# One decoder layer step: the last convolution tile beside the attention heads, no paged attention beside the fourth head, weight remainders in halves

## The chip, the cores and the metric

The kernel runs on one core of one Trainium2 chip. The core has a matrix engine (PE, with PEld for its weight loads), a vector engine (DVE), a scalar engine (ACT), a general engine (POOL) and queues for DMA, of which SP issues nearly all. Each engine works through its own instructions in a fixed order and waits on semaphores for the others. The metric is the device time of one launch in microseconds (us), the median of several runs.

## The reference

One layer of a hybrid decoder for a prompt of 1024 tokens (with 16 learned meta tokens ahead of it) and, beside it, one new token for each of 8 sequences that have 4096 tokens in a paged cache. All of it is fp32.

```python
proj = rms_norm(x, ln_mix_pre) @ w_in          # (1040, 1024) @ (1024, 2560)
q, k, v, a, g = split(proj)                    # 512 columns each
u = a * sigmoid(g)
o = softmax(q1 k1') v - lam * softmax(q2 k2') v   # 4 heads, two maps each, causal, ALiBi
y = silu(layer_norm(depthwise_conv31(u) + b))  # 512 channels, causal
x = x + rms_norm(concat(head_norm(o), y) @ w_out, ln_mix_post)
h = rms_norm(x, ln_ffn_pre)
y_prompt = x + rms_norm((silu(h @ w_gate) * (h @ w_up)) @ w_down, ln_ffn_post)
# the 8 sample rows: the same layer, with attention over k, v = cache[page_table]
```

## The kernel before

**Stages.** Every fp32 matmul is done as three matmuls of rounded parts (`mm3`, lines 149 to 151): a weight tile is cast by ACT to its upper part H (L138) and another engine subtracts H from it for the remainder L (L140). The prompt's normalised rows lie transposed in `xH`, `xL` (8 tiles of 128 channels, in three token chunks of 280, 384 and 384). Then come, on PE: the four channel tiles of the convolution group (`stripe_ag(ct)`: two projections `pa` and `pg` from weight tiles `wi12+ct` and `wi16+ct`, the sigmoid on ACT, the product u on DVE); v, q and k of head 0; 32 attention blocks, 8 for each of the 4 heads; the output projection (8 `c_block`s, matmuls `mo`); and the feed-forward part (`pg`, `pu`, `dn`), which takes the rest of the time.

**The depthwise convolution** of a channel tile (`conv_half`, two halves of 512 tokens) is 31 taps: 11 of them are multiplied on ACT (L411, L413) and added on POOL (L414), the other 20 are fused multiply-adds on DVE (L415, L423), and L421 adds the two sums. `conv_norm` (8 token blocks: transposes on PE, statistics on DVE, affine on ACT) and `conv_act` (8 pieces: transposes `zT`, then Silu on ACT, L450) follow later, and write the result to DRAM (`mixT`), from where the output projection reads it (`mx`).

**One attention block** (`attn(h, i)`): scores S on PE (L507, L508), maximum with the ALiBi bias on DVE (`nm`, L509), exponential on ACT (L515), its combination on DVE (L521 to L526), transposes `AT` on PE copied out by ACT (L538), values `o` on PE (L548), then a norm that needs a power on POOL (`or`, L564) and a scaling on ACT (L566).

**What stands beside the blocks.** A generator `chunks()` gives out the projections of the heads to come, 30 pieces, one projection of one token chunk each; the loop calls for as many as `chunk_to` says, the last one by block 22 (`fend`). `dec_step(rate)` moves the paged attention of the 8 sample rows on by so many steps; a step loads a pair of key pages, multiplies them by the query on POOL (L680, twice) and sums on DVE (L690), and later multiplies by value pages on PE (L732). `rate_b` holds a rate for each head, `rate_c` that of the output projection. `dec_max` and `dec_exp` close the scores of one sample row (`dg` is a maximum over partitions on POOL, L707; L712 subtracts it). `cn` is the block at which `conv_norm` begins, `scn` that of the sample rows' convolution. From block 27 on, two tiles of `w_out` are split for each block (`wo0` to `wo7`).

**What sets the order.** The program is written in the order of these loops, but a list scheduler of the framework places the instructions of each engine by priority (the place in the program) and by its own idea of when their inputs are ready. `conv_half` has its priority lowered by 400 places, so its multiply-adds fill in where nothing else is ready. The order of the `w_in` loads on SP is a list (`order`). There are 35 buffers of weight-tile size (`slabs`), so loads wait for buffers to come free.

Of the kernel before, what the change touches and what calls it, by code (L numbers as in the profile page):

```python
# [8 lines left out]
F32 = mybir.dt.float32  # L9
# [11 lines left out]
DB = 8  # L21
# [20 lines left out]
SLAB = 1056  # L42
OHW = P + 4
# [3 lines left out]
def tile_layer(ctx: ExitStack, tc: tile.TileContext, I, O, cfg):  # L47
# [87 lines left out]
    def load_split(src, name, l_eng, n3=True):  # L135
        raw = early.pop(name, None) or load_raw(src, name, n3)
        H = slab(name + "H", F32R)
        S.copy(H[:, :1024], raw[:, :1024])  # L138
        L = slab(name + "L", F32R)
        l_eng.tensor_tensor(L[:, :1024], raw[:, :1024], H[:, :1024].bitcast(F32), op=ALU.subtract)  # L140
        return H, L
# [43 lines left out]
    def xchunk(c):  # L185
# [11 lines left out]
        for k, pt in enumerate(pts):  # L197
            wk = wpre[:, k : k + 1]
            S.mul(xH[k][:, c0 : c0 + w], pt[:, :w], wk)
            V.scalar_tensor_tensor(  # L200
                xL[k][:, c0 : c0 + w], pt[:, :w], wk, xH[k][:, c0 : c0 + w].bitcast(F32), op0=ALU.mult, op1=ALU.subtract
            )
            if c == 0:
                V.tensor_scalar(xsT[:, k, :], pt[:, 0:DB], wk, None, op0=ALU.mult)
# [4 lines left out]
    order = [12, 16, 13, 17, 14, 18, 15, 19, 8, 0, 4, 9, 1, 5, 10, 2, 6, 11, 3, 7]  # L209
# [135 lines left out]
    def stripe_ag(ct):  # L345
# [6 lines left out]
        for c in range(3):  # L352
# [8 lines left out]
            else:  # L361
                d0 = 14 + c0 - DB
                V.tensor_tensor(ut[:, d0 : d0 + w], oa[:, :w], sg[:, :w], op=ALU.mult)

# [382 lines left out]
    def dec_units():  # L747
# [5 lines left out]
        def softmaxes(all_=False):  # L753
# [5 lines left out]
            while exped < ready and (all_ or nk >= at[exped] + cfg["elag"]):  # L759
                dec_exp(exped, st)  # L760
                exped += 1
# [510 lines left out]
    for ct in range(4):  # L1272
        stripe_ag(ct)
        conv_tail_out(ct)
        if ct == cfg["cst"]:
            att_consts()
            lam_consts()
            dec_consts()
        if ct == cfg["sq"]:
            sample_q()  # L1280
        with tc.high_priority(offset=-cfg["conv"]):
            conv_half(ct, 1)
            conv_half(ct, 0)
# [6 lines left out]
    def chunks():  # L1290
        for h in range(NH):
            if h:
# [6 lines left out]
    total = 30  # L1299
# [30 lines left out]
    for n in range(NH * NB):  # L1330
        h, i = n // NB, n % NB
        chunk_to(max(9 * h + (1 if i < 2 else 2 if i < 5 else 3), 1 + int(29 * n / cfg["fend"])))
# [58 lines left out]
    vgrp=2, fing=5, ml_g=0, fend=22, cst=0, db=3, cn=6, scn=12, wo0=27, wor=2, c0=7,  # L1391
    at=8, slabs=35, kv=4, p=6, dve_mul=0, rate_b=(1, 1.25, 1, 0.75), rate_c=1, rate_d=2.45, rate_s=2.2,
# [42 lines left out]
```

## Time and profile before

| | |
|---|---|
| three runs | 1431.78, 1434.7 and 1438.51 us; median 1434.7 |
| the profiled execution | 1440.69 us, of which the span in the trace is 1438.8 |
| mean granted clock of PE | 0.977 |
| busy in the span | PE 1357.1 us (94%), DVE 860.9 (60%), POOL 595.2 (41%), ACT 551.2 (38%) |

PE is busy 94% of the span, so a reader looks for the stretches in which it is not, and then for the engine or wait that PE waits for there. The table of stretches ([rows 1] below) does that for the part in front of the feed-forward stage. Within a stretch the rows of the timeline show single instructions: start, duration, engine, line, operation, tiles, and in square brackets how long the engine had stood idle and what ended that.

### The profile page before, as it was taken

What the parts mean: (1) busy time and instruction counts of PE and PEld (TensorE: products, weight loads), DVE (VectorE), ACT (ScalarE), POOL (GpSimd) and SP (SyncE); (2) the same over time, 40 slices, a digit from 0 to 9 for tenths busy, and PEclk for the clock granted to TensorE, in tenths of its full rate; (3) what the DMA queues carried; (4) which work ended last, traced back from release to release, by engine and by line L of the source; (5) the groups of instructions that cost most, each with busy time, mean ns of one, the idle gap of its engine ahead of it and who ended that gap; (6) DMA issues with size and microseconds to landing.
All of it is one profiled execution on the core that took longest, in us unless ns stands there. A gap on an engine that the chain in (4) does not pass through costs nothing.

```text
span 1438.8 us, 21552 instructions
## 1 busy us (share of the span) xinstructions
PE 1357.1 (94%) x6960; PEld 1057.1 (73%) x6960; DVE 860.9 (60%) x1403; ACT 551.2 (38%) x1112; POOL 595.2 (41%) x479
## 2 busy tenths in 40 slices
PE   5999899989869999999999989999999989999997
PEld 5999799979747787777776757676776765666666
DVE  5689996936684567566645465654653374452158
ACT  6566878797764345113021121312121112211122
POOL 4598867445372113745545455464530000000023
PEclk9999999999889999999999999999999999999999
DMA  8211015226535548678867857777677656763454
GB/s 246 86 59 38 27 55 163 75 96 192 170 98 193 171 148 269 211 259 260 262 226 235 265 199 249 235 257 264 204 263 221 214 163 218 229 190 125 147 195 172
DMA packets 199677, 264.34 MB, mean 184 GB/s; under 512 B 16423, under 2 KB 99816, under 8 KB 199557
## 3 DMA queue, kind: packets, MB, share of 16 engines
q1 hardware_dynamic: 188912, 254.40, 54.3%
q10 hardware_dynamic: 10653, 8.57, 1.8%
q8 instruction: 55, 0.90, 0.3%
q14 instruction: 57, 0.47, 0.1%
HBM read 245.92 MB, written 17.48 MB: 183 GB/s over the span
## 4 chain that ended last, share of the span: by engine, by line
PE 59%; SPq 3%; DMA 3%; issue 3%; DVE 3%; POOL 2%; ACT 1%; POOLq 0%; DVEq 0%; ACTq 0%
PE dn L149 5%; PE pu L149 5%; PE dn L150 5%; PE dn L151 5%; PE pu L151 5%; PE pu L150 5%; PE pg L149 5%; PE pg L150 5%; PE pg L151 5%; PE pv L732 4%; PE mo L151 2%; PE mo L149 2%; PE mo L150 2%; DMA v<-in_cache_v 2%; SPq L665 2%
## 5 line engine op out<-in xcount | busy, mean ns | idle before, releaser
L680 POOL TENSOR_TENSOR k<-k,qB 128x512 f32<-128x512 f32 x256 | 353.5, 1409 | 230.2 <-DMA k<-in_cache_k 176.3
L690 DVE TENSOR_REDUCE s<-k 128x16 f32<-128x1024 f32 x128 | 154.8, 1213 | 101.1 <-POOL k L680 100.9
L956 ACT CAST wH<-wr 128x1024 fp32r<-128x1024 f32 x66 | 69.0, 1048 | 239.4 <-DVE wL L958 124.6
L149 PE MATMUL dn<-wH,aH 128*128 128x512 f32 x352 | 141.3, 405 | 5.0 <-DVE y L999 3.4
L149 PE MATMUL pu<-hH,wH 128*128 128x512 f32 x352 | 141.2, 401 | 1.1 <-DVE y L999 1.1
L150 PE MATMUL dn<-wL,aH 128*128 128x512 f32 x352 | 140.9, 400 | 0.0
L151 PE MATMUL pu<-hH,wL 128*128 128x512 f32 x352 | 139.2, 396 | 1.6 <-DVE wL L958 1.6
L151 PE MATMUL dn<-wH,aL 128*128 128x512 f32 x352 | 140.7, 400 | 0.0
L149 PE MATMUL pg<-hH,wH 128*128 128x512 f32 x352 | 140.4, 399 | 0.0
L150 PE MATMUL pu<-hL,wH 128*128 128x512 f32 x352 | 140.1, 398 | 0.0
L150 PE MATMUL pg<-hL,wH 128*128 128x512 f32 x352 | 139.3, 396 | 0.0
L151 PE MATMUL pg<-hH,wL 128*128 128x512 f32 x352 | 139.2, 395 | 0.0
L958 DVE TENSOR_TENSOR wL<-wr,wH 128x1024 fp32r<-128x1024 f32 x66 | 93.7, 1420 | 46.3 <-ACT wH L956 22.2
L999 DVE TENSOR_TENSOR y<-dn,y 128x512 f32<-128x512 f32 x144 | 95.5, 684 | 38.0 <-PE dn L151 37.1
L414 POOL TENSOR_TENSOR cb<-cb 128x512 f32<-128x512 f32 x80 | 102.9, 1316 | 18.0 <-ACT cb L413 9.9
L1071 POOL TENSOR_TENSOR y<-y,wfpost 128x512 f32<-128x512 f32 x10 | 17.6, 1772 | 206.7 <-ACT ft L1069 206.6
L423 DVE SCALAR_TENSOR_TENSOR acc<-u,cw,acc 128x512 f32<-128x512 f32 x144 | 98.7, 747 | 0.2
L982 ACT CAST aH<-sg 128x512 fp32r<-128x512 f32 x44 | 27.3, 620 | 167.6 <-DVE sg L975 167.5
L149 PEld LDWEIGHTS dn<-wH,aH 128*128 128x128 f32 x352 | 67.5, 192 | 31.8 <-DVE y L999 6.8
L149 PEld LDWEIGHTS pu<-hH,wH 128*128 128x128 f32 x352 | 66.4, 189 | 29.4 <-issue 12.9
L975 DVE TENSOR_TENSOR sg<-sg,pu 128x512 f32<-128x512 f32 x44 | 30.1, 683 | 94.0 <-PE pu L151 94.0
L149 PEld LDWEIGHTS pg<-hH,wH 128*128 128x128 f32 x352 | 66.1, 188 | 27.4 <-issue 11.6
(581 smaller groups left out, 2969.5 us busy)
## 6 DMA issues: line engine op xcount, KB each, us to landing
k<-in_cache_k SPq DMA_DIRECT2D x256, 256.0 KB
v<-in_cache_v SPq DMA_DIRECT2D x256, 256.0 KB
wr<-in_w_gate SPq DMA_DIRECT2D x22, 512.0 KB
wr<-in_w_up SPq DMA_DIRECT2D x22, 512.0 KB
wr<-in_w_down SPq DMA_DIRECT2D x22, 512.0 KB
sd<-in_w_down SPq DMA_DIRECT2D x22, 512.0 KB
sw_gate<-in_w_gate SPq DMA_DIRECT2D x20, 512.0 KB
sw_up<-in_w_up SPq DMA_DIRECT2D x20, 512.0 KB
```

The lines of the kernel that those rows point to most:

```text
L149: T.matmul(out, lhsT=wH, rhs=xH, start=first, stop=False)
L150: T.matmul(out, lhsT=wH, rhs=xL, start=False, stop=False)
L151: mark(T.matmul(out, lhsT=wL, rhs=xH, start=False, stop=last))
L414: G.tensor_tensor(accp, accp, t, op=ALU.add)
L423: V.scalar_tensor_tensor(dst, src, cw[:, ct, k : k + 1], acc, op0=ALU.mult, op1=ALU.add)
L680: x = G.tensor_tensor(kt[:, i, :], kt[:, i, :], qB, op=ALU.mult)
L690: x = V.tensor_reduce(s.rearrange("p a c -> p (a c)"), kt.rearrange("p a (c d) -> p (a c) d", d=HD), axis=AX.X, op=ALU.add)
L732: x = T.matmul(pv[32 * g : 32 * g + 8, :], lhsT=a[:, q + i, :], rhs=vt[:, i, :], start=q + i < 4, stop=q + i >= NPG - 4, tile_position=(0, ...
L956: S.copy(H[:, :1024], raw[:, :1024])
L958: V.tensor_tensor(L[:, :1024], raw[:, :1024], H[:, :1024].bitcast(F32), op=ALU.subtract)
L975: V.tensor_tensor(sg, sg, o, op=ALU.mult)
L999: V.tensor_tensor(y[b][:, ws], o, y[b][:, ws], op=ALU.add)
```

## The change

1. The channel tile ct = 3 leaves the row of four and becomes three more pieces of `chunks()` (33 in all) ahead of the projections of head 2; its convolution follows its third piece, and its weights (15 and 19) are loaded behind tile 5.
2. `rate_b` of the last head goes from 0.75 to 0, `rate_c` from 1 to 1.75 (six steps out of the last head, six into the output projection). `dec_exp` waits for the end of the attention blocks where it isn't asked for all.
3. `conv_norm` begins at block 14 rather than 6, `conv_act` therefore at 22 rather than 14; the sample rows' convolution is called at 14 rather than 12.
4. Where POOL makes a remainder (`w_out` and all of `w_in` but tiles 8 to 12) it does so in two instructions of 512 columns.
5. The sample rows' `xsT` is made from `xH` + `xL` by eight additions behind the loop, not in it.

```diff
--- before.py
+++ after.py
@@ -40,6 +40,7 @@
 C0 = CHUNKS[0][1]
 KT = [(0, META)] + [(META + P * i, P) for i in range(NB)]
 SLAB = 1056
+LATE = {2: 3}
 OHW = P + 4
 
 
@@ -137,7 +138,9 @@
         H = slab(name + "H", F32R)
         S.copy(H[:, :1024], raw[:, :1024])
         L = slab(name + "L", F32R)
-        l_eng.tensor_tensor(L[:, :1024], raw[:, :1024], H[:, :1024].bitcast(F32), op=ALU.subtract)
+        for a in (0, 512) if l_eng is G else (0,):
+            e = a + 512 if l_eng is G else 1024
+            l_eng.tensor_tensor(L[:, a:e], raw[:, a:e], H[:, a:e].bitcast(F32), op=ALU.subtract)
         return H, L
 
     point = {}
@@ -200,13 +203,14 @@
             V.scalar_tensor_tensor(
                 xL[k][:, c0 : c0 + w], pt[:, :w], wk, xH[k][:, c0 : c0 + w].bitcast(F32), op0=ALU.mult, op1=ALU.subtract
             )
-            if c == 0:
-                V.tensor_scalar(xsT[:, k, :], pt[:, 0:DB], wk, None, op0=ALU.mult)
+        if c == 0:
+            for k in range(8):
+                V.tensor_tensor(xsT[:, k, :], xH[k][:, 0:DB].bitcast(F32), xL[k][:, 0:DB].bitcast(F32), op=ALU.add)
 
     w_in_v = I["w_in"][0].rearrange("(k p) n -> p k n", p=P)
 
     ahead = {}
-    order = [12, 16, 13, 17, 14, 18, 15, 19, 8, 0, 4, 9, 1, 5, 10, 2, 6, 11, 3, 7]
+    order = [12, 16, 13, 17, 14, 18, 8, 0, 4, 9, 1, 5, 15, 19, 10, 2, 6, 11, 3, 7]
 
     def w_in_src(ft):
         return w_in_v[:, :, ft * P : (ft + 1) * P]
@@ -361,6 +365,19 @@
             else:
                 d0 = 14 + c0 - DB
                 V.tensor_tensor(ut[:, d0 : d0 + w], oa[:, :w], sg[:, :w], op=ALU.mult)
+            if c < 2:
+                yield
+        conv_tail_out(ct)
+        if ct == cfg["cst"]:
+            att_consts()
+            lam_consts()
+            dec_consts()
+        if ct == cfg["sq"]:
+            sample_q()
+        with tc.high_priority(offset=-cfg["conv"]):
+            conv_half(ct, 1)
+            conv_half(ct, 0)
+        yield
 
 
     cw = cst.tile([P, 4, CW], F32, name="cw")
@@ -756,7 +773,7 @@
                 dec_max(ready, st)
                 at.append(nk)
                 ready += 1
-            while exped < ready and (all_ or nk >= at[exped] + cfg["elag"]):
+            while exped < ready and (all_ or kv_n[1] and nk >= at[exped] + cfg["elag"]):
                 dec_exp(exped, st)
                 exped += 1
 
@@ -1270,17 +1287,9 @@
     xchunk(2)
     conv_consts()
     for ct in range(4):
-        stripe_ag(ct)
-        conv_tail_out(ct)
-        if ct == cfg["cst"]:
-            att_consts()
-            lam_consts()
-            dec_consts()
-        if ct == cfg["sq"]:
-            sample_q()
-        with tc.high_priority(offset=-cfg["conv"]):
-            conv_half(ct, 1)
-            conv_half(ct, 0)
+        if ct not in LATE.values():
+            for _ in stripe_ag(ct):
+                pass
     att_fixed()
     for _ in stripe_v(0):
         pass
@@ -1289,6 +1298,8 @@
 
     def chunks():
         for h in range(NH):
+            if h in LATE:
+                yield from stripe_ag(LATE[h])
             if h:
                 yield from stripe_v(h)
                 yield from stripe_q(h)
@@ -1296,7 +1307,11 @@
 
     fl = chunks()
     emitted = [0]
-    total = 30
+    total = 30 + 3 * len(LATE)
+
+    def keys_at(h):
+        return 9 * h + 3 * len([x for x in LATE if x <= h])
+
 
     def chunk_to(n):
         while emitted[0] < min(n, total):
@@ -1329,7 +1344,7 @@
     nwo, ncb = 0, 0
     for n in range(NH * NB):
         h, i = n // NB, n % NB
-        chunk_to(max(9 * h + (1 if i < 2 else 2 if i < 5 else 3), 1 + int(29 * n / cfg["fend"])))
+        chunk_to(max(keys_at(h) + (1 if i < 2 else 2 if i < 5 else 3), 1 + int((total - 1) * n / cfg["fend"])))
         attn(h, i)
         if cfg["cn"] <= n < cfg["cn"] + NB:
             conv_norm(n - cfg["cn"])
@@ -1388,8 +1403,8 @@
     lag=7, rlag=1, elag=2,
     xn_g=(), wi_first=1, wi_e=(13, 17), sq=0,
     behind=-400, w0=7, w1=7, wi_n=1, anchor=1, wi_v=(8, 9, 10, 11, 12), taps=11, conv=400, r2_g=1, hb=5,
-    vgrp=2, fing=5, ml_g=0, fend=22, cst=0, db=3, cn=6, scn=12, wo0=27, wor=2, c0=7,
-    at=8, slabs=35, kv=4, p=6, dve_mul=0, rate_b=(1, 1.25, 1, 0.75), rate_c=1, rate_d=2.45, rate_s=2.2,
+    vgrp=2, fing=5, ml_g=0, fend=22, cst=0, db=3, cn=14, scn=14, wo0=27, wor=2, c0=7,
+    at=8, slabs=35, kv=4, p=6, dve_mul=0, rate_b=(1, 1.25, 1, 0), rate_c=1.75, rate_d=2.45, rate_s=2.2,
     ffn_l=lambda nc: nc.vector,
 )
 _INS = [
```

On PE, the place where the third channel tile ends. `xH`, `xL` are the prompt's rows, `pa` and `pg` the two projections of a channel tile, `pv` the v projection of a head (tile 8 belongs to head 0). Before:

```order
L149 MATMUL pg_1111<-xH_101,wi18H 128x384
L150 MATMUL pg_1111<-xL_109,wi18H 128x384
L151 MATMUL pg_1111<-xH_101,wi18L 128x384
L149 MATMUL pa_1242<-xH_94,wi15H 128x280
L150 MATMUL pa_1242<-xL_102,wi15H 128x280
L151 MATMUL pa_1242<-xH_94,wi15L 128x280
```

The same place after:

```order
L152 MATMUL pg_1116<-xH_101,wi18H 128x384
L153 MATMUL pg_1116<-xL_109,wi18H 128x384
L154 MATMUL pg_1116<-xH_101,wi18L 128x384
L152 MATMUL pv_1246<-xH_94,wi8H 128x280
L153 MATMUL pv_1246<-xL_102,wi8H 128x280
L154 MATMUL pv_1246<-xH_94,wi8L 128x280
```

The v projection of head 0 follows at once; `pa_..<-xH_94,wi15H` and what belongs to it stands further down, behind the first scores of head 1 (`S`, lines now numbered 17 higher):

```order
L524 MATMUL S_0_2425<-R_10_2188,L_10_1934 128x144
L524 MATMUL S_0_2430<-R_11_2189,L_11_1935 128x144
L152 MATMUL pa_2491<-xH_94,wi15H 128x280
L153 MATMUL pa_2491<-xL_102,wi15H 128x280
L565 MATMUL o_1894<-vm,metaT_115 128x128
L565 MATMUL o_1894<-V_1325,ats_2137 128x128 x3
L565 MATMUL o_1894<-V_1325,ats_2145 128x128 x4
L525 MATMUL S_0_2425<-R_10_2190,L_10_1934 128x144
L154 MATMUL pa_2491<-xH_94,wi15L 128x280
```

The 144 matmuls of the fourth tile's two projections have moved there from the place ahead of head 0, and lie among the instructions of attention blocks.

On ACT, a place in the last head, blocks 4 and 5 (`p`: exponentials of a block's two maps; `woNH`: casts of `w_out`; `oh`, `mo`: the norm of a finished block and its result; `u<-zT`: Silu of `conv_act`). Before:

```order
L515 ACTIVATE p_5176,l_4873<-p_5176,nm_5175 128x784
L138 CAST wo4H<-wo4r 128x1024
L515 ACTIVATE p_5185,l_4873<-p_5185,nm_5175 128x784
L566 ACTIVATE oh_4834<-oh_4834,or_4841 128x128 x4
L515 ACTIVATE p_5269,l_4873<-p_5269,nm_5268 128x912
L538 COPY metaT_117<-AT_4982 16x128
L573 ACTIVATE mo_4932<-oT_4927,sublnT 128x512
L138 CAST wo5H<-wo5r 128x1024
```

After:

```order
L467 ACT_TABLE_LOAD
L467 ACTIVATE u_2489<-zT_4741,clnb,clnw 128x512
L139 CAST wo4H<-wo4r 128x1024
L532 ACT_TABLE_LOAD
L532 ACTIVATE p_5185,l_4888<-p_5185,nm_5184 128x912
L583 ACTIVATE oh_4849<-oh_4849,or_4856 128x128 x4
L467 ACT_TABLE_LOAD
L467 ACTIVATE u_2489<-zT_4747,clnb,clnw 128x512
L532 ACT_TABLE_LOAD
L532 ACTIVATE p_5194,l_4888<-p_5194,nm_5184 128x912
L139 CAST wo5H<-wo5r 128x1024
```

Two of the eight Silus stand between exponentials there, each with an `ACT_TABLE_LOAD` ahead of it and another ahead of the next exponential. In the whole order six Silus with twelve such loads now stand behind the first exponential of the last head, and two with four just ahead of it, in blocks 6 and 7 of head 2. Before, the eight Silus and their loads stood between block 6 of head 1 and block 3 of head 2, and there was no load in the last head.

On POOL, the last head (`k`: products of the paged attention; `woNL`: remainders of `w_out`; `or`: the power in a block's norm). Before:

```order
L140 TENSOR_TENSOR wo5L<-wo5r,wo5H 128x1024
L680 TENSOR_TENSOR k_14_5090<-k_14_5090,qB_4070 128x512 x2
L140 TENSOR_TENSOR wo6L<-wo6r,wo6H 128x1024
L680 TENSOR_TENSOR k_16_5242<-k_16_5242,qB_4070 128x512
L140 TENSOR_TENSOR wo7L<-wo7r,wo7H 128x1024
L564 TENSOR_TENSOR or_5072<-ssq_4874,mhalf 128x4
L680 TENSOR_TENSOR k_16_5242<-k_16_5242,qB_4070 128x512
L564 TENSOR_TENSOR or_5433<-ssq_4874,mhalf 128x4
```

After:

```order
L143 TENSOR_TENSOR wo5L<-wo5r,wo5H 128x512 x2
L143 TENSOR_TENSOR wo6L<-wo6r,wo6H 128x512 x2
L143 TENSOR_TENSOR wo7L<-wo7r,wo7H 128x512 x2
L581 TENSOR_TENSOR or_5034<-ssq_4889,mhalf 128x4
L581 TENSOR_TENSOR or_5328<-ssq_4889,mhalf 128x4
L126 TENSOR_TENSOR zr_r<-zr_t,mhalf 128x1
L126 TENSOR_TENSOR hr_r<-hr_t,mhalf 128x1
```

The products k_14 and k_16 have left, and each remainder is two instructions. Of the eight products and four sums (L690) that stood in this head, four and two are left, both near its beginning; the value matmuls that PE did before the output projection (four) are gone from there, and the output projection has twelve in place of eight.

## Rows read from the trace of the kernel before

**Rows 1.** Stretches: length; PE, PEld, DVE, ACT, POOL busy (instructions); PE clock, DMA share, GB/s.

```profile
153.40:228.60 75.20, 68.12 (x430) 65.20 (x431) 71.21 (x157) 63.57 (x147) 50.66 (x43) 0.95 0.20 63
228.60:297.80 69.20, 68.63 (x479) 67.20 (x478) 52.23 (x132) 57.10 (x156) 38.74 (x35) 1.00 0.37 116
297.80:375.00 77.20, 70.79 (x476) 66.77 (x475) 36.81 (x92) 69.05 (x165) 39.60 (x32) 0.96 0.42 134
375.00:442.20 67.20, 44.34 (x258) 38.56 (x256) 48.70 (x118) 41.95 (x111) 33.52 (x20) 0.77 0.47 153
442.20:528.00 85.80, 85.80 (x402) 68.33 (x401) 48.01 (x85) 33.13 (x90) 18.79 (x21) 1.00 0.49 158
```

**Rows 2.** Timeline of PE: first matmuls of tile 15 and of v of head 0.

```profile
101.48 0.29 PE L149 MATMUL pa<-xH,wi15H 128*128 128x280 f32 x1
...
124.62 0.29 PE L149 MATMUL pv<-xH,wi8H 128*128 128x280 f32 x1
```

**Rows 3.** Groups on DVE to 300 us, the convolution: busy, mean ns, idle before.

```profile
L423 DVE SCALAR_TENSOR_TENSOR acc<-u,cw,acc 128x512 f32<-128x512 f32 x144 | 98.7, 747 | 0.2
...
L423 DVE SCALAR_TENSOR_TENSOR u<-u,cw,acc 128x512 f32<-128x512 f32 x8 | 5.9, 740 | 0.0
L415 DVE TENSOR_SCALAR acc<-u,cw 128x512 f32<-128x512 f32 x8 | 5.8, 746 | 0.0
L421 DVE TENSOR_TENSOR acc<-acc,cb 128x512 f32<-128x512 f32 x8 | 5.5, 690 | 4.2 <-POOL cb L414 4.2
```

**Rows 4.** Groups on DVE in head 0 (153.4 to 228.6 us).

```profile
L423 DVE SCALAR_TENSOR_TENSOR acc<-u,cw,acc 128x512 f32<-128x512 f32 x44 | 30.8, 744 | 0.0
```

**Rows 5.** Timeline of PE: the start of its work.

```profile
17.66 0.57 PE L149 MATMUL pa<-xH,wi12H 128*128 128x280 f32 x1 [3.21 <-DVE xsT L204]
```

**Rows 6.** Timeline of ACT about the first Silu.

```profile
290.60 0.51 ACT L298 CAST R<-kT 64x384 fp32r<-64x384 f32 x1
291.13 1.28 ACT L450 ACT_TABLE_LOAD   x1
292.43 0.78 ACT L450 ACTIVATE u<-zT,clnb,clnw 128x512 f32<-128x512 f32 x1
...
295.70 1.28 ACT L515 ACT_TABLE_LOAD   x1
296.99 1.17 ACT L515 ACTIVATE p<-p,nm 128x1040 f32<-128x1040 f32 x1
```

**Rows 7.** Stretches of the last head, columns as in rows 1.

```profile
375.20:424.50 49.30, 32.64 (x176) 27.31 (x174) 39.08 (x109) 31.18 (x81) 24.41 (x15) 0.76 0.42 130
424.50:442.20 17.70, 11.50 (x80) 11.05 (x80) 9.43 (x10) 10.58 (x33) 9.12 (x6) 0.81 0.64 217
```

**Rows 8.** Waits in the last head (375 to 442.2 us): in total, times, longest.

```profile
ACT p L515 <- DVE nm L509: 12.0, 4, 5.6
```

**Rows 9.** Timeline of DVE, POOL and ACT in the last head.

```profile
390.61 0.43 DVE L712 TENSOR_TENSOR s<-s,dg 128x264 f32<-128x264 f32 x1 [4.55 <-POOL dg L707]
402.27 1.22 DVE L690 TENSOR_REDUCE s<-k 128x16 f32<-128x1024 f32 x1 [4.85 <-POOL k L680]
...
429.48 2.92 POOL L140 TENSOR_TENSOR wo7L<-wo7r,wo7H 128x1024 fp32r<-128x1024 f32 x1
432.37 1.01 POOL L564 TENSOR_TENSOR or<-ssq,mhalf 128x4 f32<-128x4 f32 x1
...
433.41 1.28 ACT L566 ACTIVATE oh<-oh,or 128x128 f32<-128x128 f32 x4 [3.74 <-POOL or L564]
```

**Rows 10.** Groups on POOL: key products to 450 us, a remainder in the last head.

```profile
L680 POOL TENSOR_TENSOR k<-k,qB 128x512 f32<-128x512 f32 x51 | 66.2, 1316 | 17.8 <-DMA k<-in_cache_k 17.5
...
L140 POOL TENSOR_TENSOR wo6L<-wo6r,wo6H 128x1024 fp32r<-128x1024 f32 x1 | 2.4, 2355 | 1.0 <-ACT wo6H L138 1.0
```

**Rows 11.** The value matmuls of the paged attention: ns min/median/max, first and last start.

```profile
L732 PE MATMUL pv<-v,s x512: 589/593/1061, 423.3 to 1134.9; 128*8 128x512 f32 x171
```

## The prediction

> **What bounds the kernel now.** I read the page first (PE busy 94% of the span), then the table of stretches, then PE's and ACT's timelines where PE idles. [rows 1] are the stretches that the change touches, cut at the first score matmul of each head. From 442 us on PE has no gap, in the output projection and nearly none in the feed-forward part, so there only PE's own work counts. Head 1 is the same: PE 68.6 of 69.2 us. Head 0 is bound by DVE, 71.2 of 75.2 us (95%), since the convolution's multiply-adds run beside it [rows 4]; PE idles 7.1 us and its mean clock falls to 0.95 of full speed, 2.4 GHz. In head 2 it is ACT, 69.0 of 77.2 us. In the last head no engine is full: PE 44.3, DVE 48.7, ACT 42.0 and POOL 33.5 of 67.2 us, at clock 0.77, because no projection is left to fill in. Its length is a chain of waits: exponentials wait for maxima (12.0 us in four waits, [rows 8]), and DVE twice stands for POOL, 4.55 us for `dg` and 4.85 us for a key product [rows 9].
>
> So the tile that moves doesn't save PE any work. It can only gain where PE idles now, and must not make another engine full where it goes.
>
> **The change part by part.** The sum is made against the profiled execution, 1440.7 us, which lies 6.0 us above the median of the runs, 1434.7.
>
> *The fourth tile leaves the start.* Its matmuls stand between 101.48 and 124.62 us on PE without a gap [rows 2]; v of head 0 follows at once: -23.2 us. Its weight loads go behind tile 5 on SP, past the loads of tiles 8, 0, 4, 9, 1 and 5, which come earlier; nothing on PE waits for them in head 0 before, so I count no gain. `xsT`: the first matmul waits 3.21 us for the last of the in-loop instructions [rows 5]. It doesn't read `xsT`, so what ends its wait is the remainder made just before on the same engine; eight tiny operations leave that row. -0.3, between -1 and +0.5.
>
> *Head 0, 75.2 us.* In it DVE does 44 multiply-adds of the convolution, 30.8 us [rows 4]. A tile has 115.9/4 = 29.0 us of DVE [rows 3]; it was queued behind three others, so with one tile less, and the others begun earlier by 23 us of PE time only, the order puts some 17 us less on DVE between head 0's first scores and head 1's. DVE falls to about 54. PE then bounds: 68.1 us busy, plus one projection piece more (33 pieces spread over the 22 blocks in place of 30; 23.2/6 = 3.9 us a piece), less what the clock gives back (0.05 of 68 = 3.4): 68.6. I take 68.2, -7.0. If nothing of the idle went, +3.9; if all went and the piece hid in it, -11.
>
> *Head 1, 69.2 us.* It gives out twelve pieces where it had eleven, and three of them are double: PE +4 pieces, 15.5 us, to 84.7. To DVE come the tile's 29.0 us and some 2.8 net of other work (sums and a remainder in, three blocks of `conv_norm` out): 52.2 + 31.8 = 84.0. The two are level, and the nearest row for a stage with DVE this full is head 0: it ran DVE at 95%. 84.0/0.947 = 88.7, so +19.5. Ends: +15.5 if PE alone bounds, +31.8 if DVE's work adds on (DVE had 17 us free, but in the wrong places). ACT gets the tile's 22 multiplications, at most 0.78 each like a Silu of the same shape [rows 6], 57.1 + 17 = 74; POOL 20 additions at 1.32 like a key product [rows 10], 38.7 + 26 = 65. Both stay under 88.
>
> *Head 2, 77.2 us.* ACT loses four Silus (3.1 us) and gains the affine part of five blocks of `conv_norm`, 20 short operations by the order, under 10 us by the 0.51 of a wider cast [rows 6]. Loads of the function table stay about as many. Its PE work is even: one piece more, most of the Silus' transposes out. ACT 69 and some 5 more in 77.2: +1, between -5 and +6.
>
> *The last head, 67.2 us.* Out go two key sums on DVE, four products on POOL (4 x 1.32 us), and with them the 4.85 us wait, since the remaining product now stands ahead of the first remainder, not behind it. `dg` stays, and its wait. In come six Silus and twelve loads of the function table on ACT. The row: a load takes 1.28 us, begins as the cast before it ends (290.60 + 0.51 = 291.11) and the next function starts behind it with 0.01 us between [rows 6]. So 6 x 0.78 + 12 x 1.28 = 20.1 us. They all stand between the head's first exponential and its last; that stretch has ACT busy 31.2 of 49.3 us now [rows 7], so 51.3 after: ACT, which waits 18 us there now, becomes the engine that bounds. If waits worth another 2 us are left, the stretch is 53 (+4). In the 17.7 us behind it the key product and the 2.92 us remainder ahead of `or` shrink or go: ACT waits 3.74 us for it [rows 9], -3. With the shorter instructions on POOL, for which DVE need not stand as long, -1. Sum 0; between -9 (ACT's work falls into the waits) and +17 (none does). The convolution's part of `mixT` is now written near this head's end, and the first `mo` matmuls read it; no row of before has a wait there, and I leave it inside the +17.
>
> The Trainium skill's "ScalarE: Activation LUTs" (What ACT_TABLE_LOAD costs) speaks against this part: each switch of table costs the load and a drain, about 2.66 us. By that the twelve would be 32 us, not 15, and the last head some 17 us longer; the rows show no time for a drain, so the sum stays with the row.
>
> *Remainders in halves.* One of 1024 columns takes 2.36 us and a product of 512 columns 1.32 [rows 10]: two halves would be 2.6, +0.3 each on an engine that is 50 to 56% busy in heads 1 to 3 [rows 1]: 0, between -1 and +1 apart from the last head.
>
> *Output projection.* PE is full, so its four extra value matmuls count in whole: 4 x 0.593 = +2.4 us [rows 11]. Six steps of products and sums (POOL 6 x 2.6, DVE 6 x 1.2) lie in engines that are 22% and 56% busy. The feed-forward part does what is left of the paged attention as before: 0, within 2.
>
> Sum: -23.2 - 0.3 - 7.0 + 19.5 + 1 + 0 + 2.4 = -7.6, hence 1433.1 us against the profiled execution and, 6.0 lower, **1427** against the median.
>
> **The rivals.**
> *Exchange.* Head 1 becomes DVE-bound in whole and takes +29 (the tile's own DVE time) where I have 19.5, so that what is saved at the start is paid there: sum +2, 1437, no change. For it: head 0 shows just this with four tiles. Against it: in head 1 DVE has 17 us free, and no convolution is behind it.
> *The table loads (slower).* In the last head the Silus fall on the path of the exponentials in place of its waits: each switch pair holds back an exponential by 3.35 us, the maxima behind it wait for buffers, and the 18 us of waiting stay. +17 there, sum +9, 1444. For it: an engine works in order, and the waits come from DVE, POOL and `dg`, not from ACT. It decides once 8 us more of the 20.1 stand on the path than the 4 that I counted.
> *All gaps close.* Head 0 -11, head 1 +15.5, head 2 -3, last head -6, output projection +2.4: sum -25.6, 1409. For it: PE does no more than before and had 36 us of gaps in heads 0, 2 and 3. Against it: those of the last head come from dependences that the change leaves.
> *It doesn't do what it says.* The order keeps four products and two sums in the last head at rate 0; by this only half the paged attention leaves it. In the sum that is already so.
>
> **How the numbers follow.** 0.5% of 1434.7 is 7.2 us, about what can be told from no change: faster is under 1427.5, slower over 1441.9. Forecast 0.50 (its own range 1419 to 1436, about half of it faster by over 0.5%: 0.27 faster, 0.23 same); exchange 0.19 (0.15 same, 0.04 slower); table loads 0.17 (0.05 same, 0.12 slower); all gaps close 0.14 (faster). That gives faster 0.41, same 0.43, slower 0.16. The range 1413 to 1442 holds the forecast and the exchange, half of the two others.
>
> **What would show it.** In the profile after, v of head 0 should begin at about 101 us on PE; head 0 should take 66 to 71 us with PE over 92% busy and DVE about 55; head 1 85 to 93 us with DVE and PE both over 90%; the last head should hold twelve loads of 1.28 us on ACT, ACT about 60 of 67 us busy, and no wait of DVE for a key product over 2 us. It is wrong if head 1 is over 95 us, if the last head is over 73, or if a load on ACT comes with idle time ahead of it that nothing releases.

## The result and the profile after

The changed kernel is slower: 1459.2 us median (1457.55 to 1461.78) against 1435.7 for the kernel before beside it, a ratio of 1.0145 with a 95% interval from 1.0104 to 1.0186. That is 23.5 us more, where 7.6 less was forecast, and 17 us above the range's upper end.

The stretches of the profiled execution after (span 1455.9), cut in the same places, with columns as in [rows 1]:

```profile
126.98:198.03 71.05, 67.18 (x432) 65.63 (x433) 54.32 (x128) 53.84 (x130) 45.89 (x39) 0.98 0.22 70
198.03:307.08 109.05, 95.14 (x616) 91.96 (x615) 83.47 (x168) 72.68 (x176) 64.86 (x54) 0.95 0.33 104
307.08:381.70 74.62, 67.91 (x460) 64.49 (x460) 46.51 (x122) 63.50 (x168) 42.52 (x41) 0.96 0.25 79
381.70:456.68 74.98, 46.72 (x273) 41.66 (x271) 40.72 (x108) 67.91 (x136) 30.17 (x24) 0.75 0.39 136
456.68:543.00 86.32, 86.32 (x405) 67.91 (x404) 48.23 (x84) 32.59 (x89) 23.55 (x25) 1.00 0.55 182
```

The stages start and end at the first score matmul of a head and at the first `mo`, as before; what other work lies between two such cuts can move. Lengths in us, before (153.44, 228.59, 297.80, 375.32, 442.19 and 1438.8 are the cuts, exact to the matmul; [rows 1] rounds some of them), forecast change and measured change:

| stage | before | forecast | after | change |
|---|---|---|---|---|
| start, to the first score of head 0 | 153.4 | -23.5 | 127.0 | -26.5 |
| head 0 | 75.2 | -7.0 | 71.1 | -4.1 |
| head 1 | 69.2 | +19.5 | 109.0 | +39.8 |
| head 2 | 77.5 | +1 | 74.6 | -2.9 |
| last head | 66.9 | 0 | 75.0 | +8.1 |
| output projection to the end | 996.6 | +2.4 | 999.2 | +2.6 |

The sum is +17.0 in these two executions: the profiled one of before lay 5.0 us above its median, that of after 1.7 below. Five of the six terms lie within 4 us, or within the bounds given for them, of what was forecast; head 1 misses by 20. It is 107.5 to 109.3 us long in the profiles of all six kernels with the late tile and 35 buffers, and 69.2 to 71.2 in all seven with the tile at the start. The small terms are less certain: from profile to profile the start varies by 3 to 4 us and the last stage by 8 to 10. On PE's timeline v of head 0 begins here, where it began at 124.62 [rows 2]:

```profile
98.83 0.29 PE L152 MATMUL pv<-xH,wi8H 128*128 128x280 f32 x1
```

Head 1 splits in two halves (columns as before):

```profile
198.03:230.00 31.97, 31.97 (x223) 31.89 (x223) 11.10 (x26) 26.42 (x62) 19.17 (x17) 1.00 0.36 112
230.00:300.00 70.00, 60.55 (x375) 57.92 (x374) 65.51 (x132) 40.81 (x96) 43.49 (x35) 0.93 0.30 95
```

For 32 us PE is full and DVE works 11.1; for the next 70 DVE is nearly full (65.5) and PE works 60.6 with its clock down to 0.93. The tile's `pa` and `pg` come first, and its taps can't start before `u` is there. The timeline of DVE shows both: at 229.75 it has stood 6.09 us for a score matmul, the last product `u` follows at 230.25, and ten us later nearly every step of an attention block has a tap of 0.74 us ahead of it (L367 makes `u`, L440 is the tap, L526 the maximum).

```profile
229.75 0.57 DVE L526 CUSTOM_DVE_ANT_0 p<-S,alibi 128x400 f32<-128x400 f32 x1 [6.09 <-PE S L525]
...
230.25 0.55 DVE L367 TENSOR_TENSOR u<-pa,sg 128x384 f32<-128x384 f32 x1
...
239.09 0.42 DVE L526 CUSTOM_DVE_ANT_0 p<-S,alibi 128x264 f32<-128x264 f32 x1
239.44 0.74 DVE L440 SCALAR_TENSOR_TENSOR acc<-u,cw,acc 128x512 f32<-128x512 f32 x1
240.10 0.42 DVE L526 CUSTOM_DVE_ANT_0 p<-S,alibi 128x264 f32<-128x264 f32 x1
```

PE's waits in head 1 after (in total, times, longest); before it had one of 0.6 us there:

```profile
PE AT L551 <- DVE nm L526: 4.4, 1, 4.4
PE S L524 <- ACT R L303: 4.0, 1, 4.0
PE S L524 <- DVE L L274: 2.2, 1, 2.2
PE pk L152 <- DVE nm L526: 1.8, 1, 1.8
```

PE stands 13.9 us there in all. The 4.0 us for `R` (the keys of head 2, cast by ACT) lie at the head's end. Before, 24 matmuls of head 3's `v` stood between head 2's keys and its first score:

```profile
297.67 0.29 PE L151 MATMUL pv<-xH,wi11L 128*128 128x280 f32 x1
297.80 0.23 PE L507 MATMUL S<-R,L 128*128 128x144 f32 x1
```

After, no projection is left to put there:

```profile
307.08 0.49 PE L524 MATMUL S<-R,L 128*128 128x144 f32 x1 [4.03 <-ACT R L303]
```

By the code the loop has called for 22 of 30 pieces at block 16 before, one more than head 2's keys need, and for 24 of 33 after, just those.

PE also has more to do in head 1 than the tile. Its projection matmuls go from 265 to 361, the 96 more that four pieces are. But matmuls of attention blocks have moved in too, 16 of the values `o` from head 0's stretch and 30 from head 2's, with 15 transposes `AT`. The largest group of them before, and after:

```profile
L548 PE MATMUL o<-V,ats 128*128 128x128 f32 x46 | 6.4, 275 | 0.0
L565 PE MATMUL o<-V,ats 128*128 128x128 f32 x86 | 13.1, 305 | 0.0
```

In the last head ACT is busy 67.9 of 75.0 us. Its loads there are 15, with seven Silus, where the sum had twelve and six behind the first exponential. The loads, and a piece of the timeline: a load of the function table, the Silu, two short steps with no load ahead of them, a load, the exponential.

```profile
L532 ACT ACT_TABLE_LOAD x8 | 10.3, 1283 | 0.1
L467 ACT ACT_TABLE_LOAD x7 | 9.0, 1283 | 0.1
```

```profile
412.31 1.28 ACT L467 ACT_TABLE_LOAD   x1
413.60 0.78 ACT L467 ACTIVATE u<-zT,clnb,clnw 128x512 f32<-128x512 f32 x1
414.28 0.30 ACT L579 ACTIVATE junk<-oh 128x129 f32<-128x129 f32 x1
414.48 0.19 ACT L579 ACTIVATION_READ_ACCUMULATOR junk<-oh 128x1 f32 x1
414.69 1.28 ACT L532 ACT_TABLE_LOAD   x1
415.98 0.84 ACT L532 ACTIVATE p<-p,nm 128x656 f32<-128x656 f32 x1
```

A load costs its 1.28 us, with at most 0.02 us of idle time ahead of it and behind it in all 15, as the sum took it. The drain that the Trainium skill's "ScalarE: Activation LUTs" (What ACT_TABLE_LOAD costs) adds to it isn't in this trace: by its 2.66 us a switch the 15 loads would be an estimated 40 us, and they take 19.3.

### The profile page after: what moved, and what is told of

The parts are those of the page before. It is cut to its first block, busy times and chain, and to the rows that moved or that the text cites. A ratio compares the mean times of both kernels' runs of the same rounds, so it can differ in the third digit from the quotient of the medians.

```text
span 1455.9 us, 21588 instructions
## 1 busy us (share of the span) xinstructions
PE 1360.9 (93%) x6960; PEld 1061.4 (73%) x6960; DVE 860.8 (59%) x1403; ACT 565.0 (39%) x1124; POOL 601.9 (41%) x502
## 4 chain that ended last, share of the span: by engine, by line
PE 53%; SPq 5%; issue 4%; DMA 4%; DVE 3%; POOL 2%; ACT 1%; POOLq 0%; DVEq 0%; ACTq 0%
PE dn L152 5%; PE dn L153 4%; PE pu L152 4%; PE dn L154 4%; PE pu L154 4%; PE pu L153 4%; PE pg L152 4%; PE pg L154 4%; PE pg L153 4%; PE pv L749 3%; SPq L682 2%; SPq L676 2%; PE mo L152 2%; PE mo L153 2%; DMA k<-in_cache_k 2%
## 5 line engine op out<-in xcount | busy, mean ns | idle before, releaser
L707 DVE TENSOR_REDUCE s<-k 128x16 f32<-128x1024 f32 x128 | 155.0, 1212 | 84.7 <-POOL k L697 84.2
L973 ACT CAST wH<-wr 128x1024 fp32r<-128x1024 f32 x66 | 69.2, 1048 | 241.8 <-DVE wL L975 138.3
L431 POOL TENSOR_TENSOR cb<-cb 128x512 f32<-128x512 f32 x80 | 102.6, 1310 | 25.0 <-ACT cb L430 22.2
L440 DVE SCALAR_TENSOR_TENSOR acc<-u,cw,acc 128x512 f32<-128x512 f32 x144 | 99.7, 747 | 0.2
```

Of the source, the lines that this page charges most:

```text
L431: G.tensor_tensor(accp, accp, t, op=ALU.add)
L440: V.scalar_tensor_tensor(dst, src, cw[:, ct, k : k + 1], acc, op0=ALU.mult, op1=ALU.add)
L707: x = V.tensor_reduce(s.rearrange("p a c -> p (a c)"), kt.rearrange("p a (c d) -> p (a c) d", d=HD), axis=AX.X, op=ALU.add)
```

## The experiments

Each gives the difference to the kernel before that ran beside it, whose median was 1435.7 to 1438.1. Where a ratio says more it stands with its interval. The edits show the lines that matter; others are left out. Two changed kernels that are compared ran at different times, and the kernel before had moved by up to 2.4 us between these, so a few us between them say nothing.

**The parts alone.** The late convolution (`cn=14, scn=14` in the kernel before):

```diff
-vgrp=2, fing=5, ml_g=0, fend=22, cst=0, db=3, cn=6, scn=12, wo0=27
+vgrp=2, fing=5, ml_g=0, fend=22, cst=0, db=3, cn=14, scn=14, wo0=27
```

> The kernel before with one part of the change: conv_norm begins at block 14 and the sample rows' convolution at 14, so that the eight Silus come late (by its order eight Silus with sixteen table loads from block 7 of head 2 to block 7 of head 3). The fourth tile stays at the start, the rates are those of before. Theory A (of the 23.5 us, the last head's 8 come from the Silus and their loads on ACT, which becomes full there): the last head takes 75 to 80 us in place of 67, ACT over 65 us busy in it; head 2 loses some of its 77 us; time 1438 to 1446. Theory B (the last head got longer by the missing paged attention and the moved tile, the loads lie in waits): last head 67 to 69, time 1433 to 1437.

Measured 1435.3, ratio 0.9984 (0.9949 to 1.0020): no difference. Heads 2 and last of this run:

```profile
295.75:362.85 67.10, 62.57 (x429) 58.96 (x427) 47.61 (x125) 56.15 (x158) 39.74 (x36) 1.00 0.31 100
362.85:441.25 78.40, 50.66 (x294) 41.41 (x292) 49.07 (x113) 70.31 (x140) 32.71 (x21) 0.76 0.50 168
```

Both theories were half right. The last head does take 78 us, with ACT busy 70.3 of them; but head 2 gives back 10 of them, since the same Silus and loads are gone from there. Together the two take 145.5 us, before 144.4. The time of the whole run is theory B's, not theory A's.

The rates, the remainders with `xsT`, and the tile alone (edits as in the change's parts 2, 4 and 5, and 1 with 3):

```diff
-rate_b=(1, 1.25, 1, 0.75), rate_c=1,
+rate_b=(1, 1.25, 1, 0), rate_c=1.75,
-while exped < ready and (all_ or nk >= at[exped] + cfg["elag"]):
+while exped < ready and (all_ or kv_n[1] and nk >= at[exped] + cfg["elag"]):
```

> The kernel before with the rates alone: 0 in the last head, 1.75 in the output projection, and dec_exp gated. Theory A: the last head gets shorter by 3 to 8 us (the wait for the key product and the one at its end go, no loads come), the output projection longer by about 2.4: 1429 to 1434. Theory B (paged attention moved to where PE is full costs more than it gave): last head as before, later stages longer by 5 or more: 1438 to 1445.

Measured 1443.2, ratio 1.0038 (1.0013 to 1.0064): theory B. The last head isn't shorter (66.4 us, before 66.9). But the two waits that were to go are mostly still there, where they were 4.85 and 3.74 us [rows 9]:

```profile
DVE s L690 <- POOL k L680: 3.7, 1, 3.7
ACT oh L566 <- POOL or L564: 3.2, 1, 3.2
```

So the rates don't do there what the sum counted on, and what these waits are worth isn't shown. The median is 5 us longer. The profiled execution, the slowest of its ten, is 9.7 us longer behind the last head: PE works 2.0 us more, and of its waits the one for value pages is 3.5 us longer (from 440 us on; before: 10.9 us in six waits):

```profile
PE pv L732 <- DMA v<-in_cache_v: 14.4, 3, 8.3
```

```diff
-l_eng.tensor_tensor(L[:, :1024], raw[:, :1024], H[:, :1024].bitcast(F32), op=ALU.subtract)
+for a in (0, 512) if l_eng is G else (0,):
+    e = a + 512 if l_eng is G else 1024
+    l_eng.tensor_tensor(L[:, a:e], raw[:, a:e], H[:, a:e].bitcast(F32), op=ALU.subtract)
```

> The kernel before with the remainders on POOL in halves and the new making of xsT alone. Theory A: no difference to be told, 1433 to 1438. Rival: shorter instructions on POOL hold DVE less, the last head 2 to 4 us shorter, 1430 to 1433; or their greater number makes heads 0 and 1 longer, 1439 or more.

Measured 1441.0, ratio 1.0014 (0.9987 to 1.0041): no difference to be told, though within the profile the last head is 63.0 us. There the combining step on DVE (17 instructions) takes less than before; the rows are of before and of this run:

```profile
L526 DVE SCALAR_TENSOR_TENSOR p<-p,cc,p 128x400 f32<-128x400 f32 (+7 forms) x17 | 22.0, 1328 | 0.1
L529 DVE SCALAR_TENSOR_TENSOR p<-p,cc,p 128x400 f32<-128x400 f32 (+7 forms) x17 | 16.6, 1009 | 0.1
```

That the halves do this isn't shown: with the tile late and the remainders whole the same 17 instructions take 16.5 and 17.2 us. Heads 1 and 2 were 4 us longer in that execution, which takes the gain back.

The tile with the late convolution (parts 1 and 3, of which two lines are shown):

```diff
+LATE = {2: 3}
-cn=6, scn=12
+cn=14, scn=14
```

> The fourth tile beside head 1 with conv_norm at 14, all else (rates, remainders, xsT) as in the kernel before. Theory A (the loss is the tile's place and the late Silus): head 1 takes 105 to 112 us as in the changed kernel, the last head 75 to 80, time 1456 to 1466. Theory B (the rates or the halves are a good part of the loss): 1440 to 1450.

Measured 1466.4, +28.3 us, ratio 1.0190 (1.0121 to 1.0259). Head 1 takes 107.5 us, as theory A said, the last head 86.2, more than it said. So the tile's move, with the late convolution that it brings, is all of the loss.

With the new rates as well (parts 1 to 3):

```diff
 LATE = {2: 3}
-rate_b=(1, 1.25, 1, 0.75), rate_c=1,
+rate_b=(1, 1.25, 1, 0), rate_c=1.75,
```

> The fourth tile beside head 1 with conv_norm at 14 and the new rates, remainders whole and xsT as in the kernel before (the changed kernel without its parts 4 and 5). The run without rates took 1466.4 and 86 us in the last head, the changed kernel 1459.2 and 75. If the rates made that difference: last head 74 to 78, 1457 to 1461. If the halves did: last head 82 to 86, 1463 to 1470.

Measured 1466.2, ratio 1.0181 (1.0134 to 1.0229): the rates change nothing, and the last head has 84.3 us, the halves' side of what was expected. What is left to the changed kernel's 1459.2 is the halves and `xsT`. Head 2 and the last head together are 152.8 us here and 149.6 with the halves. The medians differ by 7 us, but against the kernel before beside each it is 28.1 and 23.5, and the two ratios' intervals overlap. That the halves are worth something beside the tile isn't shown.

**Head 1.** Three runs leave out work of the fourth tile; they have 34 buffers of weight-tile size, so a fourth gives the changed kernel with 34.

```diff
-slabs=35
+slabs=34
```

> The changed kernel with 34 weight-size buffers in place of 35 and nothing else: the measure for the runs without taps and without projections, which have 34. If the missing buffer explains why these two, with 13 and 17 us less in head 1, were no faster: 1468 to 1476, head 0 about 76 us and the feed-forward part 5 longer, head 1 still 105 to 112. If it does nothing: 1457 to 1462.

Measured 1479.6, more than was named for it. One buffer less costs 20 us, spread over the start, head 0, head 1 and the later part. Heads 0 and 1:

```profile
131.52:207.29 75.77, 69.77 (x448) 67.41 (x448) 55.17 (x128) 56.88 (x136) 47.44 (x41) 0.98 0.22 67
207.29:318.32 111.03, 95.41 (x600) 91.09 (x599) 81.69 (x168) 70.44 (x170) 62.95 (x53) 0.93 0.31 99
```

Without the taps on DVE:

```diff
-for k in range(max(n, 0) + 1, CW):
+for k in range(max(n, 0) + 1, CW) if ct != 3 else (CW - 1,):
```

> The changed kernel without 19 of the 20 taps that DVE does for the fourth tile (its output differs in those channels; 38 of its DVE instructions go, 34 weight-size buffers in place of 35). The tile's projections, ACT's and POOL's taps stay in head 1. Theory A (head 1's extra 20 us beyond my sum are DVE's: its multiply-adds start only when the whole tile is there and then stand between the attention's steps while PE waits): head 1 takes 84 to 92 us in place of 109, time 1436 to 1444. Theory B (PE's share, late keys of head 2 or table loads of the sigmoid in head 1 set it): head 1 over 102 us, time over 1452.

Measured 1464.3, against the run with 34 buffers -15.2 us. Theory A's number for head 1 was 84 to 92, theory B's over 102; it is between, the time on theory B's side, and PE nearly fills the head:

```profile
207.93:303.52 95.59, 89.75 (x601) 85.37 (x600) 58.38 (x130) 71.20 (x170) 64.71 (x54) 1.00 0.34 109
```

Its clock is 1.00 there and PE waits 6 us in all, against 0.93 and 16. Without the projections (the taps stay):

```diff
-ga, gg = proj(HA, f"pa{ct}"), proj(HG, f"pg{ct}")
+kk = 1 if ct == 3 else 8
+ga, gg = proj(HA, f"pa{ct}", kk), proj(HG, f"pg{ct}", kk)
```

> The changed kernel with the fourth tile's projections over one of eight channel groups (18 matmuls in place of 144, output differs; 34 buffers), its convolution whole. If DVE's chain alone sets head 1: it stays over 95 us, time over 1445. If it is the two together (PE 85 and DVE 84 us, badly laid beside one another): 84 to 92 us, time 1434 to 1444. If PE's share alone set it: 75 to 82.

Measured 1462.9, -16.6 us against the same. Head 1 is just past what was named for the two together:

```profile
206.35:298.57 92.22, 73.21 (x466) 66.86 (x465) 79.44 (x161) 67.20 (x162) 61.96 (x51) 0.96 0.31 98
```

Without both:

```diff
+for k in range(max(n, 0) + 1, CW) if ct != 3 else (CW - 1,):
+kk = 1 if ct == 3 else 8
```

> The changed kernel with both left out for the fourth tile: 126 of its 144 projection matmuls and 19 of the 20 taps on DVE (output differs; 34 buffers). Theory A (head 1's idle comes from the two loads lying unevenly beside one another, DVE empty first and full later): PE's 14 us of waits in head 1 are down to 4 or less and head 1 takes 70 to 78 us, against 96 and 92 us with only one left out. Theory B (the waits come from elsewhere, late keys of head 2 or the sigmoid's table loads): head 1 over 82 us with 8 us or more of waits.

Measured 1450.9, -28.6 us. Head 1:

```profile
204.01:286.78 82.77, 70.29 (x467) 65.17 (x466) 59.62 (x125) 66.49 (x162) 62.94 (x52) 1.00 0.38 121
```

Theory A named 70 to 78 us and 4 us of waits; it is 82.8 and 12.5, theory B's numbers. So A falls. PE's waits that are left are nearly all for ACT, the two largest of them here:

```profile
PE o L566 <- ACT metaT L556: 3.9, 4, 1.4
PE S L525 <- ACT R L303: 3.5, 1, 3.5
```

The second is the wait for head 2's keys again. What these four runs do show is that the two loads add: 15.2 for the taps, 16.6 for the projections, 28.6 for both. The sum, 31.8, agrees with 28.6 within the spread of the last run (ten from 1440.9 to 1456.2, the profiled one the fastest). Each shows only in part: the 38 taps are 28 us of DVE's time, and PE is busy 22.2 us less without the projections. But if they had run side by side, taking one away would have given little.

Two guesses on the rest. The sigmoid's table loads:

```diff
-S.activation(sg[:, :w], og[:, :w], AF.Sigmoid)
+S.activation(sg[:, :w], og[:, :w], AF.Sigmoid if ct != 3 else AF.Identity)
```

> The changed kernel with the identity in place of the sigmoid for the fourth tile (output differs): four table loads less among the exponentials of head 1, 5.1 us of ACT. If part of head 1's length comes from them: head 1 103 to 106 us in place of 109, time 1453 to 1457. If they lie in waits: 108 to 110, 1458 to 1461.

Measured 1460.6 with head 1 at 108.3 us: they lie in waits. The place of the tile:

```diff
-LATE = {2: 3}
-order = [12, 16, 13, 17, 14, 18, 8, 0, 4, 9, 1, 5, 15, 19, 10, ...]
+LATE = {1: 3}
+order = [12, 16, 13, 17, 14, 18, 8, 0, 4, 15, 19, 9, 1, 5, 10, ...]
```

> The changed kernel with the fourth tile one head earlier, beside head 0 (34 buffers, so to be compared with the run that has 34 and is otherwise the changed kernel, 1479.5). Theory A (the tile costs its PE and DVE work wherever PE is already full): head 0 about 105 to 112 us in place of 76, head 1 72 to 78 in place of 111, time 1472 to 1482. Theory B (head 1 is a bad place, by the order of that head): the two together 175 to 180 in place of 187, time 1462 to 1471.

Measured 1463.7, -15.8 us against the run with 34 buffers, theory B's side. Heads 0 and 1:

```profile
129.56:227.70 98.14, 88.65 (x547) 84.85 (x547) 86.72 (x171) 75.22 (x158) 73.25 (x60) 0.95 0.21 63
227.70:307.06 79.36, 74.80 (x507) 71.77 (x508) 57.13 (x128) 56.06 (x157) 40.48 (x36) 1.00 0.33 104
```

Together 177.5 us, not 186.8. The place matters by about 9 us in these two heads; at either place they are far above the 144.4 us that they took with the tile at the start (and 35 buffers).

**The loads in the last head.** The changed kernel with a function ahead of which no load stands:

```diff
-S.activation(u[ct][:, a : a + 512], pt, AF.Silu, scale=clnw[...], bias=clnb[...])
+S.activation(u[ct][:, a : a + 512], pt, AF.Identity, scale=clnw[...], bias=clnb[...])
```

> The changed kernel with the identity in place of Silu in conv_act (output differs): the order stays, but no table is loaded in the last head (sixteen loads and none of the eight operations less). Theory A (the loads set the last head's 75 us, ACT being busy 68 of them): last head 62 to 67 us, time 1447 to 1452. Theory B (the loads lie in waits, as the late convolution alone cost nothing in sum): last head 72 to 75, time 1456 to 1460.

Measured 1446.7, 12.5 us less than the changed kernel, theory A. Head 2 and the last head:

```profile
310.08:383.78 73.70, 68.04 (x459) 64.86 (x460) 45.83 (x119) 62.61 (x168) 42.56 (x41) 0.95 0.25 81
383.78:447.49 63.71, 43.72 (x273) 39.39 (x271) 42.17 (x112) 47.68 (x120) 30.83 (x24) 0.84 0.46 159
```

The sixteen loads are 20.5 us of ACT; some 12 us of that stood on the path (11.3 in the last head's length). The wait behind it, DVE for the exponential, in the changed kernel and here:

```profile
DVE rl L538 <- ACT p L532: 16.0, 5, 8.2
DVE rl L538 <- ACT p L532: 3.7, 3, 1.7
```

The same result without loads, by tanh, beside which the trace has no load in the last head:

```diff
-S.activation(u[ct][:, a : a + 512], pt, AF.Silu, scale=clnw[...], bias=clnb[...])
+S.activation(th, pt, AF.Tanh, scale=hw, bias=hb)        # hw, hb: half of clnw, clnb
+V.tensor_scalar(u[ct][:, a : a + 512], pt, hw, hb, op0=ALU.mult, op1=ALU.add)
+V.scalar_tensor_tensor(u[ct][:, a : a + 512], th, 1.0, u[ct][:, a : a + 512], op0=ALU.add, op1=ALU.mult)
```

> The changed kernel with Silu by tanh: no table load in the last head, but two operations more on DVE for each of the eight pieces. By the run with the identity (last head 64 us, 1446.7) and 11 us more of DVE there: last head 64 to 70, time 1447 to 1453. If DVE pays it back in whole, as in the kernel before with tanh: last head 73 to 80, 1456 to 1462.

Measured 1461.4. The gain is gone in whole, as the second expectation said; the last head:

```profile
383.60:460.71 77.11, 51.00 (x275) 43.53 (x274) 53.92 (x128) 48.82 (x121) 32.40 (x24) 0.69 0.38 126
```

ACT has 19 us less, DVE 13 more, and the head is 2 us longer. The trace shows where it goes. In total PE waits longest for DVE's first new step, which reads `zT`; with the identity PE waits 0.6 us ahead of `zT`. One such wait is shown below the total:

```profile
PE zT L468 <- DVE u L477: 12.7, 6, 4.1
414.51 1.11 PE L468 MATMUL zT<-ident,u 128*128 128x128 f32 x4 [4.06 <-DVE u L477]
```

The kernel has one buffer for `zT` (`nd=1`), and with tanh DVE holds it until its step has run. So it is the place of DVE's steps in a chain, and not only their 13 us, that takes the gain back. A second buffer for `zT` wasn't tried, so how much is the buffer's and how much DVE's time stays open.

Three versions meant to be faster, all on the kernel before: tanh with the late convolution,

```diff
-cn=6, scn=12
+cn=14, scn=14
+S.activation(th, pt, AF.Tanh, scale=hw, bias=hb)
```

> A version meant to be faster: the kernel before with conv_norm at 14 (as in the run with the late convolution alone) and Silu as z/2 (1 + tanh(z/2)), whose table is that of the exponential, with two operations more on DVE for each of the eight pieces; by its order no load stands among the exponentials but that of the sample rows. Theory A: head 2 keeps its 67 us and the last head falls from 78 to 64 to 69: 1422 to 1429. Theory B (loads cost nothing there): 1434 to 1437.

measured 1438.7, ratio 1.0006 (0.9987 to 1.0025), last head 80.0 us; the same with the new rates,

```diff
-rate_b=(1, 1.25, 1, 0.75), rate_c=1,
+rate_b=(1, 1.25, 1, 0), rate_c=1.75,
```

> A version meant to be faster: the kernel before (fourth tile at the start) with conv_norm at 14, Silu by tanh, and the rates of the change (0 and 1.75). In the run with tanh the last head took 80 us since paged attention, tanh pieces on DVE and the attention blocks share it; in the changed kernel without loads it took 64. If the paged attention is what is left there: head 2 67 us, last head 62 to 68, feed-forward part up to 8 longer: 1424 to 1434. If not: last head 75 or more, 1436 to 1446.

measured 1441.9, ratio 1.0040 (1.0012 to 1.0068), last head 80.2; and tanh with the convolution where it was,

```diff
 cn=6, scn=12
+S.activation(th, pt, AF.Tanh, scale=hw, bias=hb)
```

> The kernel before with Silu by tanh alone, conv_norm still at 6: eight loads of the table less beside head 2, where ACT is busy 69 of 77 us; sixteen operations more on DVE, which has 40 us free there. If the loads are what head 2 waits for: head 2 70 to 73 us, 1429 to 1434. If they lie in waits: 1434 to 1439.

measured 1446.7, ratio 1.0049 (1.0019 to 1.0079), with head 2 at 88.9 us in place of 77.5. All three expectations of a gain failed. What they share is the two operations more on DVE for each piece. The same chain stands in their traces: ACT waits for `zT` 6.5, 4.1 and 16.9 us in the heads named. No run takes that wait away, so for the three the cause is argued. No version here beats the kernel before.

## Why the prediction was wrong, point by point

- *The fourth tile leaves the start: -23.5.* Right. The pair of profiles gives -26.5, but the start is 151.2 to 154.1 us in all seven profiles with the tile there and 127.0 to 131.2 in the six without it (35 buffers). The rows give the tile 23.14 us, not 23.2.
- *Head 0: -7.* Smaller, -4.1. DVE fell to 54.3 us as said, PE is busy 67.2 of 71.1. Part of the 4.1 isn't a gain: 16 of its `o` matmuls now stand in head 1. With 34 buffers they stay, and the head takes 75.8 us.
- *Head 1: +19.5.* This step failed. The prediction put PE at 84.7 and DVE at 84.0 us, called them level, and stretched DVE's by the share that head 0 had shown (0.947) to 88.7. DVE came out as summed, 83.5. PE is busy 95.1 and stands 13.9, so of the 20.3 us that were missed 10.4 are PE's busy time and 9.9 its waits, for which the sum had 4.0. The busy time was mis-sized since it counted the projections alone. The attention matmuls that moved in and the clock (0.95 for 1.00) are the rest; without the taps PE is busy 89.8 us at a clock of 1.00 for 601 matmuls in place of 616, so by estimate each is about half. The waits were mis-sized since the two loads were taken to run side by side. The runs show that they add: the tile's taps cost 15.2 us and its projections 16.6 where they stand, 28.6 together. Head 0 of before was a wrong measure for it, since the last of its taps belonged to a tile whose matmuls had ended at 124.6 us, 29 us ahead of the head; in head 1 the taps wait for the tile's own matmuls, so DVE stands 21 of the first 32 us and is nearly full afterwards, while PE waits for DVE's maxima (6.2 us) and loses clock.
- *What the sum for head 1 left out.* The 4.0 us for head 2's keys, at the head's end, weren't in it. And with neither load 83 us remain, against 69.2 before: PE is busy 1.7 us more and waits 11.9 more, nearly all of it for ACT, which still does the tile's 22 multiplications and which the sum left out as not full. No run takes ACT's part away. One buffer less is at most 6.7 us (heads 0 and 1, 186.8 and 180.1 us); the sigmoid's loads are not it.
- *The exchange rival* (+29 in head 1, 1437) named the stage and came nearer, at a chance of 0.19, and was 11 us short in price. Its mechanism, a head bound by DVE in whole, isn't what the runs show: DVE is busy 83.5 of 109 us, and without the taps the head still takes 95.6.
- *Head 2: +1; last head: 0.* The parts were mis-sized against each other: ACT in the last head is 67.9 us busy where about 60 was said (three loads and a Silu more, 4.6 us of it), and the head 8.1 us longer. The table loads are 12 us on the path (identity in place of Silu), where the sum had 4 for the whole ACT stretch, which holds the Silus too. The 3 us that it counted off at the head's end [rows 9] aren't seen: the wait for `or` is 3.2 us with the rates alone, 5.3 with the halves alone, for 3.74; in the changed kernel it is 1.1, in a head that the loads lengthen. *The slower rival* (1444, the table loads) was right in its place and sign, and alone too small: the head is 8.1 us longer for its 17, and with the tile at the start head 2 gives the loss back.
- *Remainders in halves: 0, -1 in the last head.* Alone no difference to be told, as said; beside the tile none is shown.
- *Output projection to the end: +2.4.* Measured +2.6, and that it agrees so well is luck: the stage is 991 to 999 us in the six profiles with the old rates and 996 to 1006 in the seven with the new ones (35 buffers). It has 28.6 us of PE's gaps before, so "nearly none" was a loose reading.

A fault of method ahead of that: the gain was booked as PE's gaps closing, 7 us in head 0, against a table in which heads 0 and 1 had 7.7 us of gaps in all. PE's work did not change, so the most that the move could give in these heads was that; and they have 17.8 after.

## What to carry to other kernels

When two engines' loads are moved into a stage together and one of them feeds the other, add them until a run shows that they overlap; the larger of the two is the best case, not the likely one. Count also what else moves across the cuts between stages, and whether the next stage's inputs still come early enough: here both were left out. Before work is moved to where "DVE has 17 us free", look at when these come: time that is free before the producer is done is no use. And whether a wait goes is read from the trace of the part alone; here two that were booked as gone had shrunk by 1.2 and 0.5 us.

## What was not expected

One weight-size buffer less, 34 for 35, cost 20 us (1479.6 against 1459.2), nearly as much as the change itself; a run that alters the number of buffers to make room for an experiment needs its own control. Table loads are 1283 ns each, and cost 12 of 20.5 us on the path in a stage where ACT was busy 91%; four of them in head 1 cost nothing that could be told. And two DVE operations for each of eight pieces, 13 us by the busy time, cancelled 19 us off ACT in a stage where DVE was busy 54%: PE stood 12.7 us for the first of the two.
